# Moving the pools' subtraction of the token from VectorE to GpSimd, with rescaled operands, in an encoder layer

## The chip, the cores and the metric

The kernel runs on one core of one Trainium2 chip. The metric is the device time of one execution in microseconds (us), the median of several runs. One execution was also profiled, and all rows of the trace below come from that one. Engines: PE is TensorE, DVE is VectorE, ACT is ScalarE, POOL is GpSimd, SP issues transfers. Each engine works through its own queue in order. A difference of 0.2% is about 1.8 us here.

## The reference, cut to what matters

One layer on 512 tokens of 1024 channels, all in float32. The middle of it is a mixing block between two feed-forward blocks:

```python
h = h + 0.5 * swiglu(rms_norm(h, ffn1_norm[l]), ...)
u = rms_norm(h, mix_norm[l]) @ w_in[l]
q, k, v, pc = jnp.split(u, ...)          # 512 | 128 | 128 | 512 columns
a = window_attention(q, k, v, sink_logits[l])
p = multiscale_pool(pc, pool_w[l], pool_scale[l])
h = h + jnp.concatenate([a, p], axis=-1) @ w_out[l]
h = h + 0.5 * swiglu(rms_norm(h, ffn2_norm[l]), ...)
...
def multiscale_pool(u, w_pool, pool_scale):      # four groups of 128 channels, w = 2, 4, 8, 16
        means.append(0.5 * (win_mean(t - half, t + half - 1) + win_mean(t - half + 1, t + half)))
    d = (mean - uf).reshape(B, S, N_POOL_GROUPS, POOL_GROUP_WIDTH)
    y = jnp.einsum('bsgc,gcd->bsgd', d, w_pool.astype(jnp.float32)).reshape(B, S, POOL_WIDTH)
    return (y * pool_scale.astype(jnp.float32)).astype(u.dtype)
```

## The kernel before

Channels lie on the 128 partitions and the 512 tokens along a row. Every float32 product is made of three matmuls (`mm3`, lines 119 to 121): each operand is split into a rounded part and a rest, as `wh` and `wl` for weights and `pdh` and `pdl` for the pools. Weights stream from memory in units; ACT rounds (line 93), and for the two projections of the mixing block the rest is made by a negation (ACT at line 97 or POOL at line 99) and a transfer that POOL issues and that adds the raw weights (line 101).

The mixing block lies between about 376 and 515 us of the span. Its projections come in the order k and v, the pool of window 16, q0, the pool of window 8, q1, q2, q3, and the pools of window 4 and 2. I call a pool by its window: pool 16, pool 8, pool 4 and pool 2 (`gi` 3 to 0). A pool goes through these steps:

- `uu` (line 423): DVE takes the projected token off PSUM and multiplies it with the norm's factor.
- `widen` and `scale` (lines 430 to 439): POOL adds shifted copies, one step per doubling of the window, corrects a few columns at either edge, and adds the two half windows into `dd`.
- `less_token` (line 442): DVE forms `dd * 0.5 / w - uu`.
- `halves` (lines 446 and 447): ACT rounds `dd` into `pdh`, DVE subtracts for `pdl`.
- `pool_linear` (lines 460 to 464): PE multiplies with the pool's weights, ACT and DVE scale by `pool_scale` and split again.

These steps are put in a list per pool (`later`) and taken off one at a time, one after each step of the work that PE does meanwhile (`eased`); `AFTER` empty steps lie between the sum and the subtraction. The attention is woven in between: scores of a block of 128 queries on PE (lines 523 and 524), the row's extreme on DVE (line 525), the exponential on ACT (528), the division on POOL (535), transposes on PE (552), their split on ACT and DVE (556 and 557, `ph` and `pl`), products on PE (567 and 568). PSUM has eight banks, so the PE can run some eight scores ahead of DVE. The order in which instructions stand in each engine's queue is fixed when the program is built, by a scheduler that departs from the order of the code in places.

Of the kernel before, what the change touches and what calls it, by code (L numbers as in the profile page):

```python
# [11 lines left out]
ALU = mybir.AluOpType  # L12
# [3 lines left out]
S = 512  # L16
# [7 lines left out]
NEG = -1e30  # L24
F0 = 3
WARM = 10
AFTER = 11
EARLY = 12
LAG = 4
POOL_W = (2, 4, 8, 16)  # L30
PAD = 8
# [3 lines left out]
def encoder_layer(ctx: ExitStack, tc: tile.TileContext, xT, w1h, w1gu, w1d, win, wout, w2h, w2gu, w2d,  # L35
                  gains, gfin, sinks, poolw, pscale, cosT, sinT, edges, out):
    nc = tc.nc
# [8 lines left out]
    def cut(a, n):  # L46
        return small[:, a:a + n]
# [98 lines left out]
    nc.gpsimd.dma_start(sink[:, 0, :], sinks)  # L146
    psc = cut(40, 4)
    nc.gpsimd.dma_start(psc, pscale)
    ident = base.tile([P, P], F32, name="ident")
    make_identity(nc, ident)  # L150
    epsb = cut(48, 1)
# [171 lines left out]
    with tc.tile_pool(name="mix", bufs=1) as mp:  # L323
# [89 lines left out]
        later = []  # L413

        def pool_means(gi, ps):
            w = POOL_W[gi]
            half = w // 2
            e0 = 2 * (half - 1)
            uu = mp.tile([P, S + 128], F32, name="uu", tag="pl", bufs=3)[:, :S + 2 * PAD]
            n = S + 2 * PAD  # L420
            nc.gpsimd.memset(uu[:, :PAD], 0.0)
            nc.gpsimd.memset(uu[:, n - PAD:], 0.0)
            nc.vector.tensor_tensor(uu[:, PAD:PAD + S], ps, rstd, op=ALU.mult)
            box = {"cur": uu}

            def widen(step):
                m = n - 2 * step + 1
                cur = box["cur"]
                nxt = mp.tile([P, S + 128], F32, name="s1", tag="s1", bufs=2)
                nc.gpsimd.tensor_tensor(nxt[:, :m], cur[:, :m], cur[:, step:step + m], op=ALU.add)  # L430
                box["cur"] = nxt

            def scale():
                cur, o = box["cur"], PAD - half
                for a, e in ((o, e0), (o + S + 1 - half, e0 + half)):
                    nc.gpsimd.tensor_tensor(cur[:, a:a + half], cur[:, a:a + half], edge[:, e:e + half],
                                            op=ALU.mult)
                box["dd"] = mp.tile([P, S], F32, name="dd", tag="ph", bufs=3)
                nc.gpsimd.tensor_tensor(box["dd"], cur[:, o:o + S], cur[:, o + 1:o + 1 + S], op=ALU.add)  # L439

            def less_token():
                nc.vector.scalar_tensor_tensor(box["dd"], box["dd"], 0.5 / w, uu[:, PAD:PAD + S],
                                               op0=ALU.mult, op1=ALU.subtract)

            def halves():
                nc.scalar.copy(pdh[:, gi, :], box["dd"])
                nc.vector.tensor_tensor(pdl[:, gi, :], box["dd"], pdh[:, gi, :].bitcast(F32),
                                        op=ALU.subtract)

            wait = [lambda: None]  # L450
            steps = []
            while 1 << len(steps) < w:
                steps.append(lambda step=1 << len(steps): widen(step))
            later.append(steps + [scale] + (AFTER - len(steps)) * wait + [less_token, halves])

        def pool_linear(gi):
            while later[3 - gi]:
# [10 lines left out]
        def projected(gi):  # L468
            steps = project(pc[gi])
            last = steps.pop()  # L470
            return steps + [lambda: (last(), pool_means(gi, pc[gi]["ps"]))]
# [14 lines left out]
        nc.vector.tensor_tensor(sr, sr, rstd, op=ALU.mult)  # L486
        keys()
        pool_means(3, pc[3]["ps"])
        vT = mp.tile([P, 4, 4 * P], F32, name="vT", tag="sc", bufs=4).rearrange("p i c -> p (i c)")[:, :S]
        nc.vector.tensor_tensor(vT, bv["ps"], rstd, op=ALU.mult)  # L490
# [307 lines left out]
```

## Time and profile before

| what | value |
|---|---|
| median of 3 runs | 896.76 us (896.28 to 897.34) |
| the profiled execution | 895.57 us |
| its span, first to last instruction | 893.8 us |
| PE busy in the span | 872.9 us (98%) |
| DVE, ACT, POOL busy | 397.2, 320.2, 313.4 us |

The page shows PE busy in nearly every slice of the span; the two slices where it falls to seven tenths lie in the mixing block. The span is 1.8 us shorter than the time of its execution, and that execution is 1.2 us below the median.

### The profile page before, as it was taken

The numbers are of one execution on the slowest core, as the hardware profiler recorded it, in microseconds if no ns is written. First come the engines' busy times: TensorE is split into PE (matmuls) and PEld (weight loads), VectorE is DVE, ScalarE is ACT, GpSimd is POOL, SyncE is SP. The second block draws the span as 40 slices with busy tenths as digits, with TensorE's granted clock in tenths as the row PEclk, the third lists the DMA queues.
The fourth block names the chain that finished last, engine by engine and source line by source line (L and its number), as shares of the span: only waits on it lengthen the run. The fifth ranks groups of instructions, "written<-read, shape, count | busy, mean of one in ns | idle before, by whom it ended". The sixth has DMA issues, their size and how long they took to land.

```text
span 893.8 us, 9718 instructions
## 1 busy us (share of the span) xinstructions
PE 872.9 (98%) x3918; PEld 720.9 (81%) x3918; DVE 397.2 (44%) x505; ACT 320.2 (36%) x464; POOL 313.4 (35%) x274
## 2 busy tenths in 40 slices
PE   9999999999999999999779999999999999999996
PEld 7888888888888888778658888888888888888885
DVE  6444444444422221548697543444444444322225
ACT  7253223332221112754666542443332232211123
POOL 5086444444410000836643320663334444200004
PEclk9999999999999999999899999999999999999998
DMA  6422222222222223585613332222222222322202
GB/s 236 160 76 95 99 98 105 105 106 100 94 95 95 95 94 113 135 212 134 140 57 70 96 118 100 89 95 95 94 95 95 95 94 95 124 98 106 105 16 94
DMA packets 17276, 94.23 MB, mean 105 GB/s; under 512 B 2112, under 2 KB 2640, under 8 KB 8400
## 3 DMA queue, kind: packets, MB, share of 16 engines
q1 hardware_dynamic: 13104, 81.60, 25.6%
q0 software_dynamic: 2688, 9.46, 5.4%
q10 hardware_dynamic: 1440, 2.57, 0.9%
q8 instruction: 30, 0.49, 0.2%
q14 instruction: 14, 0.11, 0.0%
HBM read 82.08 MB, written 2.10 MB: 94 GB/s over the span
## 4 chain that ended last, share of the span: by engine, by line
PE 88%; POOL 4%; DVE 3%; DMA 2%; issue 2%; ACT 1%; DVEq 0%; ACTq 0%; POOLq 0%; SPq 0%
PE ps L119 28%; PE ps L120 28%; PE ps L121 28%; POOL s L430 1%; DMA raw<-in_win 1%; PE ps L552 1%; DVE yl L165 1%; PE ps L568 1%; DMA wl<-raw 1%; PE ps L567 1%; POOL wl L101 1%; DVE h L306 1%; DMA small<-in_gains 0%; POOL dd L439 0%; PE ps L660 0%
## 5 line engine op out<-in xcount | busy, mean ns | idle before, releaser
L93 ACT CAST wh<-raw 128x1024 fp32r<-128x1024 f32 (+2 forms) x153 | 156.3, 1024 | 406.9 <-PE ps L120 329.0
L103 DVE TENSOR_TENSOR wl<-raw,wh 128x1024 fp32r<-128x1024 f32 (+2 forms) x135 | 201.3, 1494 | 193.3 <-ACT wh L93 192.1
L119 PE MATMUL ps<-zh,wh 128*128 128x512 f32 x346 | 135.5, 392 | 0.0
L120 PE MATMUL ps<-zl,wh 128*128 128x512 f32 x346 | 135.1, 390 | 0.0
L121 PE MATMUL ps<-xh,wl 128*128 128x512 f32 x346 | 134.9, 390 | 0.0
L119 PE MATMUL ps<-xh,wh 128*128 128x512 f32 x346 | 134.8, 390 | 0.0
L121 PE MATMUL ps<-zh,wl 128*128 128x512 f32 x346 | 134.8, 390 | 0.0
L120 PE MATMUL ps<-xl,wh 128*128 128x512 f32 x346 | 134.6, 389 | 0.0
L213 POOL TENSOR_TENSOR t<-t,t 128x512 f32<-128x512 f32 x44 | 77.6, 1767 | 146.9 <-ACT t L212 146.9
L215 POOL TENSOR_TENSOR t<-t,rstd 128x512 f32<-128x512 f32 x44 | 61.2, 1395 | 99.3 <-DVE t L214 99.3
L214 DVE TENSOR_TENSOR t<-ps,t 128x512 f32<-128x512 f32 x44 | 30.4, 691 | 120.2 <-PE ps L121 108.2
L119 PEld LDWEIGHTS ps<-xh,wh 128*128 128x128 f32 x346 | 64.9, 188 | 14.0 <-ACT wh L93 0.3
L121 PEld LDWEIGHTS ps<-zh,wl 128*128 128x128 f32 x346 | 64.9, 188 | 13.8 <-issue 0.2
L121 PEld LDWEIGHTS ps<-xh,wl 128*128 128x128 f32 x346 | 64.9, 188 | 13.8 <-issue 0.2
L120 PEld LDWEIGHTS ps<-zl,wh 128*128 128x128 f32 x346 | 65.0, 188 | 13.5 <-issue 0.2
L120 PEld LDWEIGHTS ps<-xl,wh 128*128 128x128 f32 x346 | 64.9, 188 | 13.5
L119 PEld LDWEIGHTS ps<-zh,wh 128*128 128x128 f32 x346 | 65.0, 188 | 13.3
L211 DVE TENSOR_TENSOR t<-ps,rstd 128x512 f32<-128x512 f32 x44 | 30.2, 690 | 92.4 <-PE ps L121 75.9
L119 PE MATMUL ps<-a1h,wh 128*128 128x512 f32 x176 | 68.5, 389 | 0.0
L120 PE MATMUL ps<-a1l,wh 128*128 128x512 f32 x176 | 68.5, 389 | 0.0
L121 PE MATMUL ps<-a1h,wl 128*128 128x512 f32 x176 | 68.5, 389 | 0.0
L101 POOL DMA_DIRECT2D wl<-raw x18 | 15.7, 872 | 124.3 <-ACT wl L97 120.0
(191 smaller groups left out, 1291.3 us busy)
## 6 DMA issues: line engine op xcount, KB each, us to landing
raw<-in_w1gu SPq DMA_DIRECT2D x19, 1024.0 KB, 4.7
raw<-in_w2gu SPq DMA_DIRECT2D x19, 1024.0 KB, 4.8
raw<-in_w1d SPq DMA_DIRECT2D x11, 1024.0 KB, 4.8
raw<-in_w2d SPq DMA_DIRECT2D x11, 1024.0 KB, 4.7
wl<-raw POOLq DMA_DIRECT2D x18, 512.0 KB, 4.5
raw<-in_win SPq DMA_DIRECT2D x5, 1024.0 KB, 4.8
raw<-in_wout SPq DMA_DIRECT2D x4, 1024.0 KB, 5.2
raw<-in_w2h SPq DMA_DIRECT2D x4, 768.0 KB, 4.3
```

Of the source, the lines that this page charges most:

```text
L93: nc.scalar.copy(wh[:, c:c + m], src[:, c:c + m])
L101: nc.gpsimd.dma_start(wl[:, c:c + m], src[:, c:c + m], accum_op=ALU.add)
L103: nc.vector.tensor_tensor(wl[:, c:c + m], src[:, c:c + m], wh[:, c:c + m].bitcast(F32), op=ALU.subtract)
L119: nc.tensor.matmul(ps, lhsT=ah, rhs=bh, start=start, stop=False)
L120: nc.tensor.matmul(ps, lhsT=ah, rhs=bl, start=False, stop=False)
L121: nc.tensor.matmul(ps, lhsT=al, rhs=bh, start=False, stop=stop)
L165: nc.vector.scalar_tensor_tensor(xl[:, k, :], h[:, k, :], g, xh[:, k, :].bitcast(F32), op0=ALU.mult, op1=ALU.subtract)
L211: nc.vector.tensor_tensor(t1, pg, rstd, op=ALU.mult)
L213: nc.gpsimd.tensor_tensor(t2, t2, t1, op=ALU.mult)
L214: nc.vector.tensor_tensor(t1, pu, t2, op=ALU.mult)
L215: nc.gpsimd.tensor_tensor(t1, t1, rstd, op=ALU.mult)
L306: nc.vector.scalar_tensor_tensor(h[:, i, :], ps, 0.5, h[:, i, :], op0=ALU.mult, op1=ALU.add)
```

## The change

The subtraction of the token goes from DVE to POOL. [...] The pool's scale at the end is multiplied by `1 / (2 w)` instead, once, on four columns at the start. The subtraction stands directly behind the sum in the pool's list, and 22 steps lie between the sum and `halves` where there were 11 up to the subtraction (the widening steps count in both).

```diff
-AFTER = 11
+AFTER = 22
...
     nc.gpsimd.dma_start(psc, pscale)
+    for i, w in enumerate(POOL_W):
+        nc.gpsimd.tensor_scalar(psc[:, i:i + 1], psc[:, i:i + 1], 0.5 / w, 1.0, op0=ALU.mult, op1=ALU.mult)
...
             def less_token():
-                nc.vector.scalar_tensor_tensor(box["dd"], box["dd"], 0.5 / w, uu[:, PAD:PAD + S],
-                                               op0=ALU.mult, op1=ALU.subtract)
+
+                nc.gpsimd.tensor_scalar(uu[:, PAD:PAD + S], uu[:, PAD:PAD + S], 2.0 * w, 1.0,
+                                        op0=ALU.mult, op1=ALU.mult)
+                nc.gpsimd.tensor_tensor(box["dd"], box["dd"], uu[:, PAD:PAD + S], op=ALU.subtract)
...
-            later.append(steps + [scale] + (AFTER - len(steps)) * wait + [less_token, halves])
+            later.append(steps + [scale, less_token] + (AFTER - len(steps)) * wait + [halves])
```

Lines of the changed kernel are two higher from line 149 on and four higher from line 443 on. The queues move at three places.

The first place is ACT's queue behind the projection of q0 (`vv` is the values, `qq` the queries). Before:

```order
L97 ACTIVATE wl<-wh 128x1024
L395 ACTIVATE qq<-u 64x512 x2
L406 CAST vv<-ps 128x4x64
L446 CAST pdh<-dd 128x512
L93 CAST wh<-raw 128x1024
L446 CAST pdh<-dd 128x512
L97 ACTIVATE wl<-wh 128x1024
```

And after the change:

```order
L97 ACTIVATE wl<-wh 128x1024
L450 CAST pdh<-dd 128x512
L397 ACTIVATE qq<-u 64x512 x2
L408 CAST vv<-ps 128x4x64
L93 CAST wh<-raw 128x1024
L450 CAST pdh<-dd 128x512
L97 ACTIVATE wl<-wh 128x1024
```

The rounding of pool 16 now stands ahead of the queries q0. The rounding of pool 8 keeps its place.

The second place is DVE's queue at the first scores (`uu` here is pool 4's, the rows of line 525 are the extremes of the first scores). Before:

```order
L396 SCALAR_TENSOR_TENSOR qq<-u,qq 64x512 x2
L423 TENSOR_TENSOR uu<-ps,rstd 128x512
L525 ISA sc,st<-ps,mask,small 128x256
L525 ISA st 128x1
L525 ISA sc,st<-ps,mask,small 128x256
L525 ISA st 128x1
L442 SCALAR_TENSOR_TENSOR dd<-dd,uu 128x512
L525 ISA sc,st<-ps,mask,small 128x256
L525 ISA st 128x1
L447 TENSOR_TENSOR pdl<-dd,pdh 128x512
L525 ISA sc,st<-ps,mask,small 128x256
```

And after the change:

```order
L398 SCALAR_TENSOR_TENSOR qq<-u,qq 64x512 x2
L425 TENSOR_TENSOR uu<-ps,rstd 128x512
L529 ISA sc,st<-ps,mask,small 128x256
L529 ISA st 128x1
L529 ISA sc,st<-ps,mask,small 128x256
L529 ISA st 128x1
L529 ISA sc,st<-ps,mask,small 128x256
L529 ISA st 128x1
L451 TENSOR_TENSOR pdl<-dd,pdh 128x512
L529 ISA sc,st<-ps,mask,small 128x256
```

The subtraction is gone from between the second and the third extreme. The split `pdl` of pool 4, which needs the finished `dd`, still stands ahead of the fourth.

The third place is POOL's queue at pool 2 (line 535, later 539, is the attention's division, 439 and 441 the pool's sum). Before:

```order
L436 TENSOR_TENSOR s_2980<-s_2980,edge 128x1 x2
L535 TENSOR_SCALAR sc<-sc,st 128x384
L439 TENSOR_TENSOR dd<-s_2980 128x512
L535 TENSOR_SCALAR sc<-sc,st 128x384 x3
L516 COPY sc<-small 128x4
L535 TENSOR_SCALAR sc<-sc,st 128x384 x4
```

And after the change:

```order
L438 TENSOR_TENSOR s_2985<-s_2985,edge 128x1 x2
L539 TENSOR_SCALAR sc<-sc,st 128x384
L441 TENSOR_TENSOR dd<-s_2985 128x512
L539 TENSOR_SCALAR sc<-sc,st 128x384 x3
L445 TENSOR_SCALAR uu<-uu 128x512
L520 COPY sc<-small 128x4
L539 TENSOR_SCALAR sc<-sc,st 128x384
L447 TENSOR_TENSOR dd<-dd,uu 128x512
L539 TENSOR_SCALAR sc<-sc,st 128x384 x3
```

The scaling and the subtraction of pool 2 stand among the divisions, and four divisions now lie between the sum and the subtraction.

## Rows read from the trace of the kernel before

**Rows 1.** The page: span, and busy time of each engine.

```profile
span 893.8 us, 9718 instructions
...
PE 872.9 (98%) x3918; PEld 720.9 (81%) x3918; DVE 397.2 (44%) x505; ACT 320.2 (36%) x464; POOL 313.4 (35%) x274
```

**Rows 2.** Waits of PE from 370 to 520 us: total, times, longest.

```profile
PE ps L568 <- DVE pl L557: 4.9, 1, 4.9
PE ps L523 <- DVE st L525: 4.9, 2, 4.5
```

**Rows 3.** Timeline of PE: start, us, what, idle before and its releaser.

```profile
430.97 0.40 PE L121 MATMUL ps<-yh,wl 128*128 128x512 f32 x1
435.88 0.69 PE L523 MATMUL ps<-kk,qq 128*128 128x384 f32 x1 [4.51 <-DVE st L525]
...
437.25 0.69 PE L523 MATMUL ps<-kk,qq 128*128 128x384 f32 x1 [0.37 <-DVE st L525]
...
452.01 0.80 PE L568 MATMUL ps<-pl,vz 128*128 128x512 f32 x1 [4.92 <-DVE pl L557]
...
455.38 0.43 PE L567 MATMUL ps<-ph,vv 128*128 128x512 f32 x1
...
461.52 0.47 PE L119 MATMUL ps<-pdh,wh 128*128 128x512 f32 x1
...
470.50 0.39 PE L119 MATMUL ps<-pdh,wh 128*128 128x512 f32 x1
```

**Rows 4.** Timeline of DVE.

```profile
413.03 0.69 DVE L442 SCALAR_TENSOR_TENSOR dd<-dd,uu 128x512 f32<-128x512 f32 x1 [0.93 <-POOL dd L439]
...
417.45 1.40 DVE L396 SCALAR_TENSOR_TENSOR qq<-u,qq 64x512 fp32r<-64x512 f32 x2 [0.70 <-ACT qq L395]
...
428.50 0.69 DVE L423 TENSOR_TENSOR uu<-ps,rstd 128x512 f32<-128x512 f32 x1
...
434.73 0.69 DVE L442 SCALAR_TENSOR_TENSOR dd<-dd,uu 128x512 f32<-128x512 f32 x1 [4.73 <-POOL dd L439]
...
446.89 4.47 DVE L442 SCALAR_TENSOR_TENSOR dd<-dd,uu 128x512 f32<-128x512 f32 x1 [1.13 <-POOL dd L439]
...
461.29 0.61 DVE L525 CUSTOM_DVE_ANT_0 sc<-ps,mask,small 128x384 f32<-128x384 f32 x1
...
461.83 0.61 DVE L525 CUSTOM_DVE_ANT_0 sc<-ps,mask,small 128x384 f32<-128x384 f32 x1
```

**Rows 5.** Timeline of POOL.

```profile
9.08 1.34 POOL L176 TENSOR_TENSOR acc<-acc,sq 128x512 f32<-128x512 f32 x1 [5.38 <-ACT sq L175]
...
399.36 4.68 POOL L430 TENSOR_TENSOR s<-s 128x525 f32<-128x525 f32 x3
...
411.53 1.47 POOL L439 TENSOR_TENSOR dd<-s 128x512 f32<-128x512 f32 x1
...
433.65 1.04 POOL L439 TENSOR_TENSOR dd<-s 128x512 f32<-128x512 f32 x1
...
442.03 1.06 POOL L99 TENSOR_SCALAR wl<-wh 128x1024 fp32r<-128x1024 f32 x1
...
446.56 1.93 POOL L535 TENSOR_SCALAR sc<-sc,st 128x384 f32<-128x384 f32 x3
...
448.38 2.43 POOL L535 TENSOR_SCALAR sc<-sc,st 128x384 f32<-128x384 f32 x4
```

**Rows 6.** Timeline of ACT.

```profile
435.45 0.62 ACT L446 CAST pdh<-dd 128x512 fp32r<-128x512 f32 x1 [3.39 <-DVE dd L442]
...
458.94 0.68 ACT L462 ACTIVATE pdh<-ps,small 128x512 fp32r<-128x512 f32 x1
```

**Rows 7.** Stretches: busy time of each engine, granted clock of TensorE, DMA share, GB/s.

```profile
435.90:442.00 6.10, 5.73 (x16) 4.93 (x17) 5.90 (x24) 5.44 (x19) 3.69 (x8) 0.52 0.46 94
...
452.00:456.00 4.00, 3.99 (x11) 3.29 (x12) 4.00 (x7) 2.35 (x5) 0.00 (x0) 0.57 0.16 68
```

**Rows 8.** A stretch further on in the mixing block, same columns.

```profile
464.00:480.00 16.00, 16.00 (x90) 13.50 (x90) 12.83 (x36) 11.89 (x33) 9.00 (x18) 1.00 0.03 5
```

## The prediction, made before the changed kernel ran

> **What bounds the kernel now.** I read the page first. PE is busy for 872.9 of 893.8 us [rows 1], so at most 21 us of the span can be won, and only where PE stands still or runs slow. The waits of PE in the mixing block come next: two long ones, each behind DVE, 4.9 us for the products' `pl` and 4.9 us, in two pieces, for the extremes of the scores [rows 2]. In the timeline of PE they lie at 431.37 (the end of the row at 430.97) to 435.88, with 0.37 us more before 437.25, and before 452.01 [rows 3]. I call them the first and the second wait. The reader is to see in the timeline of DVE what held DVE there. At the first wait DVE stood at pool 4's subtraction for 4.73 us, until POOL had summed; the third extreme, which frees PE's bank, is queued behind it. At the second wait pool 2's subtraction took 4.47 us where the others take 0.69 [rows 4]. All of that time POOL ran divisions without a gap [rows 5].
>
> Behind each wait PE's clock falls: 0.52 of full speed granted from 435.9 to 442 and 0.57 from 452 to 456 [rows 7], that is, mostly 1.2 GHz instead of 2.4 after PE stood idle. From 464 to 480 us PE is busy all the time [rows 8]. So the question is when PE gets to the first matmul of the output projection, at 461.52, and from there to the common point at 470.50 [rows 3]. The nine us between hold the same matmuls in both kernels, in another order.
>
> The sum is of differences, against the profiled execution of 895.57 us (span 893.8 and 1.8 around it); the median is 1.19 us above it, and I add the same difference to the median. The measurement tells a difference from none at about 0.2%, 1.8 us.
>
> **Prices.** The change removes four DVE subtractions, 0.69 us each when quiet. It adds to POOL four scalings of 128x512 and four subtractions. A division of 384 columns takes 0.61 us (2.43 for four) and a scaling of 1024 takes 1.06 [rows 5], so 512 columns cost about 0.70 by their line. A two-input operation on POOL takes 1.04 when DVE is quiet (pool 4's sum) and 1.47 beside DVE (pool 8's) [rows 5]; both ends stay in the range. I take 1.04, because DVE now has nothing to do behind the sums but wait for them. The four scalings of a 128x1 column stand ahead of POOL's first sum of squares, before which POOL idles for 5.38 us until ACT has squared [rows 5]; I cost them at nothing, and without that cover they would be less than 4 x 0.70 = 2.8 us on POOL alone.
>
> **First part: pools 16 and 8.** POOL now does two scalings and two subtractions more before pool 8's `dd` is final: 2 x 0.70 + 2 x 1.04 = 3.48 us. Against that the widening adds of pool 16 took 1.56 each (4.68 for three) where 1.04 is the quiet price [rows 5], and they may go quiet as DVE and ACT now stand at pool 16's rounding, queued ahead of the queries. I take back one such excess, 0.55: 2.93 us. What follows is shorter than before. Before, from the sum's end (411.53 + 1.47 = 413.00) to the end of the queries q1 on DVE (417.45 + 1.40 = 418.85) went 5.85 us [rows 4, 5]: DVE's subtraction and then the whole rotation. Now the rotation has already begun, and behind pool 8's subtraction only the rounding on ACT (0.62 [rows 6]), `pdl` and the last add of the rotation (0.69 each), ACT's queries (the 0.70 of idle) and 1.40 on DVE are left [rows 4]: 4.10. So the queries q1 end 2.93 - 1.75 = 1.2 us later. The rotations of q2 and q3 and pool 4's `uu` (428.50 [rows 4]) follow one behind the other on DVE and shift alike. Bounds: all four adds go quiet, nothing is late (0); none does and both subtractions cost 1.47, 4.34 - 1.75 = 2.6 us late. The transfer for the last projection's weights, which ACT's negation behind pool 8's rounding releases, is late too; PE would wait under 2 us there, and that lies inside the first wait.
>
> **Second part: pool 4 and the first scores.** The third extreme no longer waits, so PE does one score more. But the fourth stands behind `pdl` of pool 4, and `pdl` behind ACT's rounding, and that behind POOL. From the sum's end (433.65 + 1.04 = 434.69) to PE's score at 437.25 went 2.56 us [rows 3, 5]. Now 0.70 and 1.04 are added on POOL and 0.69 is gone from DVE: 1.05 us more. The wait is not removed: it moves by one score, and it ends 1.2 + 1.05 = 2.25 us later than before. DVE is idle there, so the quiet price holds.
>
> **Third part: pool 2 and the products.** In times of before (to which 2.25 is added): POOL reaches the end of three divisions at 448.38, then scales (0.70), divides once (0.61) and subtracts (1.04): 450.73. ACT rounds `pdh` (0.62) and then the fourth `ph` (as much): 451.95, and PE's fourth product can go at 452.0 where it went at 455.38 [rows 3, 5]. So 3.4 us come back here, not 4.9: ACT now waits where DVE did. Part of it is lost again. Pool 2's own linear map needs `pdl`, which DVE does behind five extremes: from 452.0 DVE has six operations of at most 0.69 and five extremes 0.54 apart (461.29, 461.83 [rows 4]), 6.8 us, so PE gets `pdl` at 458.8. PE's two matmuls, some 0.5 us, ACT's scaling (0.68 [rows 6]) and the hops bring the output projection to 460.1, against 461.52: 1.4 us earlier. From there the same matmuls follow.
>
> **Sum:** +2.25 - 1.4 = +0.85 us; with the clock left as it is, because one long wait goes from 4.9 to some 6.5 us and the other from 4.9 to two shorter ones, I forecast about 0.7 more than before: 896.3 for a profiled execution, 897.5 us for the median, no change that can be measured.
>
> **Rivals.** *Faster, the waits hidden (0.13).* POOL goes quiet, nothing is late in the first part, and extremes and split run so early that only the fourth `ph` counts: PE's 6.1 us from 455.38 to 461.52 [rows 3] shrink by their idle and slow time to some 5.3 and start at 452.0, so 457.3, 4.2 earlier; with the 1.05 of pool 4, 3.2 us are won: 893.6. For it speaks that DVE is free of its 4.47 us; against it, that `pdl` stands where it stands in DVE's queue. *Faster, the second wait simply goes (0.05):* 4.92 us and 4.0 x 0.43 = 1.7 us of slow clock [rows 3, 7], 6.6 in all, 890.2. Against it speaks that ACT must round pool 2 ahead of the fourth `ph`.
>
> *Slower, POOL beside DVE (0.31).* The subtractions of pools 16 and 8 run beside the queries and the values on DVE at 1.47, as pool 8's sum did [rows 5]; the first part is late by 2.6 and pool 4 by 1.05, 3.65 together, and pool 2's path is 0.43 longer, so only 1.0 comes back: +2.65, 899.4, and up to 1.5 more if the clock also falls behind the new waits. It decides from 2.2 us of delay in the first part on.
>
> The slower rival has a page behind it. The Trainium skill (GPSIMD Engine Reference, Engine selection) keeps elementwise work on VectorE, since two-input operations on GpSimd are about half as fast; this case's rows show 1.04 against 0.69, half as long again rather than double. By the page an estimate for one subtraction is 1.38, and four of them on the path make the sum some 1.4 us longer, 898.9. The same page (Key points) says that GpSimd shares its SBUF interfaces with VectorE and collides with DVE instructions of two SBUF inputs; the 4.47 us beside POOL's divisions agree.
>
> **Chances.** The forecast has 0.51, with its own range from 895.0 to 898.5. Faster by more than 0.2%: 0.13 + 0.05 and a little of the forecast's lower edge, 0.19. Slower: 0.31. Within: 0.50. Eight times in ten the time should lie from 893.9 to 900.3; this leaves out the fastest rival, part of the other and the slowest tail.
>
> **What the profile would show.** Right: DVE without line 442's rows; the long wait of PE at the scores one score later, over 6 us, ending 2 us later in the span; ACT idle behind POOL's subtraction of pool 16, 4 and 2; PE waiting at the fourth product on ACT's `ph` and before the output projection on `pdl` or `pdh`. POOL's scaling at 0.7 and its subtraction near 1.04. Wrong: a first wait that ends no later than before, which the quiet POOL would do; no wait for pool 2's `pdl`; or subtractions of 1.5 us and more.

## The result: 4.6 us slower, and the profile after

The changed kernel takes 901.36 us (median of 4 runs, 900.73 to 901.93) against 896.8 for the kernel before (4 runs): a ratio of 1.0051, 95% interval 1.0033 to 1.0068. The forecast was 897.5, with a range up to 900.3. The profiled execution took 900.73 us.

The page of the changed kernel, the lines that answer to [rows 1]:

```profile
span 899.0 us, 9715 instructions
...
PE 875.9 (97%) x3918; PEld 723.8 (81%) x3918; DVE 393.4 (44%) x501; ACT 321.0 (36%) x464; POOL 321.1 (36%) x286
```

PE has the same 3918 matmuls, but is busy 3.0 us longer: the same work ran at a lower clock for longer (the mean granted clock of the execution is 0.987, against 0.992 before). DVE lost its four subtractions, and POOL got twelve instructions: four on the columns of `pool_scale`, and for each pool a multiplication of the token by `2 w` and its subtraction from the unscaled sum. The waits of PE in the mixing block (370 to 525 us; total, times, longest), against [rows 2]:

```profile
PE ps L527 <- DVE st L529: 6.9, 1, 6.9
PE ps L571 <- ACT ph L560: 2.5, 1, 2.5
PE ps L121 <- DMA wl<-raw: 2.2, 2, 1.1
PE ps L120 <- DVE pdl L451: 2.1, 1, 2.1
PE ps L119 <- ACT pdh L466: 0.8, 1, 0.8
```

The first wait grew from 4.9 to 6.9 us. The second shrank from 4.9 to 2.5, and two new ones came, for pool 2's `pdl` and for its scaled `pdh`. Of the two waits for weights (`wl<-raw`), one was there before; the other ends at 422.68, ten us ahead of the first wait, which takes it up, as the prediction had it. They lie in the timeline of PE as follows, against [rows 3]:

```profile
432.93 0.34 PE L528 MATMUL ps<-kl,qq 128*128 128x384 f32 x1
440.13 0.69 PE L527 MATMUL ps<-kk,qq 128*128 128x384 f32 x1 [6.86 <-DVE st L529]
...
455.32 0.50 PE L571 MATMUL ps<-ph,vv 128*128 128x512 f32 x1 [2.46 <-ACT ph L560]
...
462.85 0.53 PE L120 MATMUL ps<-pdl,pwh 128*128 128x512 f32 x1 [2.10 <-DVE pdl L451]
...
464.63 0.80 PE L119 MATMUL ps<-pdh,wh 128*128 128x512 f32 x1 [0.83 <-ACT pdh L466]
...
475.69 0.40 PE L119 MATMUL ps<-pdh,wh 128*128 128x512 f32 x1
```

The first wait ends 2.88 us later than before (440.13 against 437.25), the output projection starts 3.11 later (464.63 against 461.52), and the common point is 5.19 later (475.69 against 470.50). That is the whole difference of the spans, 5.2. So 2.9 us were lost before the first wait ended, 0.2 on the way to the output projection, and 2.1 in the nine us behind it, where the prediction saw nothing. The stretches of the changed kernel show what that is (length; busy time and count of PE, PEld, DVE, ACT, POOL; granted clock; DMA share; GB/s), against [rows 7]:

```profile
440.00:446.00 6.00, 5.87 (x18) 5.48 (x19) 5.66 (x25) 5.89 (x20) 4.78 (x10) 0.50 0.00 1
...
456.40:459.80 3.40, 3.40 (x12) 3.19 (x11) 2.59 (x6) 2.10 (x5) 0.00 (x0) 0.50 0.00 0
459.80:463.20 3.40, 1.30 (x9) 0.90 (x7) 3.40 (x11) 3.07 (x9) 0.00 (x0) 1.00 0.00 0
463.20:470.00 6.80, 5.97 (x21) 4.43 (x20) 4.19 (x12) 3.91 (x11) 4.69 (x9) 0.50 0.01 2
470.00:475.69 5.69, 5.69 (x31) 4.56 (x30) 3.67 (x8) 3.17 (x7) 0.19 (x1) 1.00 0.00 0
```

In the mixing block the clock stood at 1.2 GHz (0.50) in three stretches, where the kernel before had two. The new one, 463.2 to 470, is the longest and lies where before PE ran at full clock [rows 8]. Ahead of it PE had 1.30 us of work in 3.40, because of the wait of 2.10.

### The profile page after: what moved, and what is told of

Same layout as the page of the kernel before. It is cut to its first block, busy times and chain, and to the rows that moved or that the text cites. A ratio compares the mean times of both kernels' runs of the same rounds, so it can differ in the third digit from the quotient of the medians.

```text
span 899.0 us, 9715 instructions
## 1 busy us (share of the span) xinstructions
PE 875.9 (97%) x3918; PEld 723.8 (81%) x3918; DVE 393.4 (44%) x501; ACT 321.0 (36%) x464; POOL 321.1 (36%) x286
## 4 chain that ended last, share of the span: by engine, by line
PE 87%; POOL 5%; DVE 3%; DMA 2%; ACT 2%; issue 1%; DVEq 0%; ACTq 0%; POOLq 0%; SPq 0%
PE ps L119 28%; PE ps L121 28%; PE ps L120 28%; POOL s L432 1%; DMA raw<-in_win 1%; PE ps L556 1%; DVE yl L167 1%; DMA wl<-raw 1%; POOL dd L447 1%; PE ps L571 1%; POOL wl L101 1%; DVE h L308 0%; PE ps L572 0%; POOL dd L441 0%; DMA small<-in_gains 0%
```

## The theories and what tells them apart

All kernels behind the common point are alike: from there to the end of the span it is 423.2 to 423.3 us in every trace. So three distances, taken inside one trace, say where a kernel gains or loses: from the first matmul of the norm's sums (385.64 us before, 385.76 after) to the end of the first wait; from there to the first matmul of the output projection; from there to the common point. For the kernel before these are 437.25 - 385.64 = 51.61, 24.27 and 8.98.

| kernel | median us | ratio to before, 95% | to the end of the first wait | to the output projection | to the common point |
|---|---|---|---|---|---|
| before | 896.8 | | 51.61 | 24.27 | 8.98 |
| changed | 901.36 | 1.0033 to 1.0068 | 54.37 | 24.50 | 11.06 |
| 1: no scaling | 897.6 | 1.0005 to 1.0022 | 52.88 | 22.42 | 11.35 |
| 2: only pool 2 | 897.38 | 1.0002 to 1.0020 | 51.55 | 25.11 | 10.56 |
| 3: all but pool 2 | 899.15 | 1.0021 to 1.0048 | 54.54 | 24.20 | 8.97 |
| 4: zero matmuls, late | 897.51 | 1.0006 to 1.0024 | 54.39 | 23.68 | 8.35 |
| 5: split 11 behind | 897.61 | 1.0003 to 1.0023 | 54.71 | 22.80 | 8.99 |
| 6: before, split 22 | 900.08 | 1.0029 to 1.0055 | 51.62 | 28.06 | 10.01 |
| 7: before, zero matmuls | 892.86 | 0.9945 to 0.9969 | 51.63 | 21.73 | 8.97 |
| 8: only pool 2, zero matmuls | 893.36 | 0.9953 to 0.9977 | 51.68 | 22.76 | 8.38 |
| 9: split 11, zero matmuls | 894.35 | 0.9975 to 0.9993 | 54.55 | 19.71 | 8.89 |
| 10: only pool 2, split 11, zero matmuls | 891.29 | 0.9935 to 0.9963 | 51.49 | 20.23 | 8.92 |
| 11: before, zero matmuls, first wait | 891.83 | 0.9936 to 0.9961 | 51.84 | 19.38 | 8.97 |
| 12: before, zero matmuls, second wait | 895.08 | 0.9982 to 1.0000 | 51.61 | 23.69 | 9.00 |

The distances are of one profiled execution each; that of the kernel before is 1.2 us under its median, so differences of the traces come out about that much larger than those of the medians. Part of the spread lies ahead of the mixing block: the norm's first matmul comes at 385.37 to 385.95 us in ten of the fourteen traces and at 386.78 to 387.13 in the other four (experiments 4, 5, 10 and 11). The distances leave that out, the medians don't.

**Theory A**: POOL's chain (scale, subtract) is longer than DVE's was, and PE waits for its end. **Theory B**: the split 22 steps behind, which puts pool 2's `pdl` behind the extremes on DVE, is what costs. **Theory C**: the clock that falls behind the new waits is the larger part.

## The experiments

**1. Without the scaling.**

```diff
-                nc.gpsimd.tensor_scalar(uu[:, PAD:PAD + S], uu[:, PAD:PAD + S], 2.0 * w, 1.0,
-                                        op0=ALU.mult, op1=ALU.mult)
```

> The changed kernel without POOL's four scalings of the token by 2w (this leaves out the factor 2w, so the pools are computed otherwise); PE, ACT and DVE keep the order of the changed kernel. Theory A (POOL's longer chain is what PE waits for): the scalings of pools 16, 8 and 4 (1.05 + 0.95 + 0.62 us) stand ahead of the first wait and that of pool 2 (0.62) ahead of the fourth product; the first wait ends about 2.6 us earlier, the whole is 898.5 us (897.5 to 899). Theory B (the later rounding and the new order are the cause, POOL's price is hidden): within 0.7 us of the changed kernel, 901.4. Theory C (the clock is the larger part, and shorter waits keep it up): below 897.

Measured: 897.6 us, 3.8 less than the changed kernel, in the range of theory A. The timeline of PE:

```profile
438.77 0.69 PE L527 MATMUL ps<-kk,qq 128*128 128x384 f32 x1 [6.16 <-DVE st L529]
...
459.64 0.50 PE L120 MATMUL ps<-pdl,pwh 128*128 128x512 f32 x1 [2.10 <-DVE pdl L451]
...
461.19 0.79 PE L119 MATMUL ps<-pdh,wh 128*128 128x512 f32 x1 [0.83 <-ACT pdh L466]
```

The first wait ends 1.5 us earlier (52.88 against 54.37) and not 2.6: where the scalings go, the widening adds take longer (three of pool 16 took 4.69 us, and 1.51 + 2.76 with the scaling among them), and with the other adds they eat 1.1 of the 2.6. Another 2.1 us come in the second distance, from pool 2. There more has changed than the scaling: in POOL's queue the subtraction stands directly behind three divisions, and the fourth, which stood ahead of it, comes behind it. So the 2.1 us are not the scaling's price alone. But the waits for `pdl` and `pdh` are still there, with the same 2.10 and 0.83, and so is the long last distance, 11.35. POOL's price is real, and it is not what makes the last two us.

**2 and 3. Pool 2 alone, and all but pool 2.** The pools in `ON` take the new way, the others the old one with 11 steps.

```diff
+ON = (0,)
...
+                if gi in ON:
+                    nc.gpsimd.tensor_scalar(uu[:, PAD:PAD + S], uu[:, PAD:PAD + S], 2.0 * w, 1.0,
+                                            op0=ALU.mult, op1=ALU.mult)
+                    nc.gpsimd.tensor_tensor(box["dd"], box["dd"], uu[:, PAD:PAD + S], op=ALU.subtract)
+                else:
+                    nc.vector.scalar_tensor_tensor(box["dd"], box["dd"], 0.5 / w, uu[:, PAD:PAD + S],
+                                                   op0=ALU.mult, op1=ALU.subtract)
```

> Only pool 2's subtraction on POOL and its rounding 22 steps behind; pools 16, 8 and 4 as in the kernel before. Theory A with the clock: first and second part as before; the fourth product comes earlier, but PE then waits for pool 2's pdl and pdh and runs at the lower level behind them, so 2.3 us are lost (5.2 less the 2.9 that the changed kernel was late at the first wait): 899.1 us. The prediction's third part without a fall of the clock: 1.4 us are won, 895.4 us.

> Pools 16, 8 and 4 on POOL and rounded 22 steps behind; pool 2 as in the kernel before. Theory A: the first wait ends 2.9 us later as in the changed kernel, the second wait is the old one: 896.8 + 2.9 = 899.7 us. Rival (the delay of the first wait is made up at the second, because pool 2's sums don't depend on it): about 897.5.

Measured: 897.38 and 899.15 us. With all but pool 2 the loss stands in the first distance alone (54.54, and 24.20 and 8.97 as before), and the median is near theory A's 899.7. With pool 2 alone the first distance is that of before, and the other two are 0.84 and 1.58 us longer: in the trace 2.4 us, as expected, in the medians only 0.6, far from the 899.1 expected. The profiled execution is 0.5 us above its median and that of the kernel before 1.2 below its own, which makes up nearly all of the difference. The profiled execution shows a mean granted clock of 0.989, as one other of this kernel does, and eight show 0.990 to 0.993: in most of them TensorE spent less time at 1.2 GHz than in the trace. So what pool 2 alone costs stays open between 0.6 and 2.4 us. Both readings are against the 1.4 us of gain that the prediction's third part gave to pool 2. And as pools 16, 8 and 4 are split 22 steps behind in the third experiment too, without harm to the last distance, it is pool 2's split that matters there.

**4. PE kept at work in the late waits.** Matmuls that add zero (one of their operands is the mask's middle block, which is all zero) go into the same bank: 8 ahead of the fourth product and 8 inside pool 2's linear map. Ahead of the output projection stand 3 of the kernel's warming matmuls, whose result the first matmul of the projection overwrites. None adds anything to a sum.

```diff
+    def idle_turns(ps, n, stop=False):
+        for j in range(n):
+            nc.tensor.matmul(ps[:, 0:P], lhsT=ones, rhs=box0["zero"], start=False, stop=stop and j == n - 1)
...
+                if n == 0 and x == 3:
+                    idle_turns(po[g], 8)
...
+            if gi == 0:
+                idle_turns(pp, 8)
...
+                if d == 0 and i == 0 and bh is pdh:
+                    keep_awake(ws[1], 3)
```

> The changed kernel with matmuls that add zero while PE waits for the fourth product and for pool 2's pdl, and 3 of the warming ones before the output projection; the first wait as it is. If the clock's fall behind these waits costs time (theory C): the stretch from the first matmul of the output projection, 6.8 us at 1.2 GHz, is nearly 2.7 us shorter: 898.7 us (898 to 899.5). If PE's speed there is hidden by ACT and DVE: 901.4 within 0.7.

Measured: 897.51 us, 3.85 less, and below the range expected of theory C (898 to 899.5). The stretch from the output projection to the common point:

```profile
465.20:473.55 8.35, 8.35 (x47) 6.85 (x47) 6.26 (x15) 5.96 (x15) 3.96 (x9) 1.00 0.00 0
```

The clock is 1.00 and the stretch 8.35 us instead of 11.06: 2.7 less, the number that theory C gave. Here the split and POOL's chain are those of the changed kernel, so this is time that the clock took: 2.1 us of it, if one goes by the kernel before, where the same distance takes 8.98 at full clock. The scheduler also moved one product, two transposes and one rounding on ACT, and the other 0.6 may be theirs. The middle distance is 0.82 shorter; in this trace the clock is 1.00 from 456 us on, so the fall behind the wait for `ph` is gone too. The first wait and its slow stretch were left alone (54.39 against 54.37).

**5. The split 11 steps behind again**, subtraction and scaling on POOL.

```diff
-AFTER = 22
+AFTER = 11
```

> The changed kernel with the split 11 steps behind again (subtraction and scaling stay on POOL). Only the last stretch is ordered otherwise: pool 2's pdl stands ahead of the extremes on DVE and its linear map ahead of the scores on PE. If the later split caused the third loss (PE's wait for pdl, 2.1 us, for pdh, 0.8 us, and the lower clock behind them, some 2 us): the first wait ends as in the changed kernel, both later waits go, 897 us (896 to 898). If POOL's price alone is the cause: within 0.7 of 901.4.

Measured: 897.61 us, 3.75 less, as expected. The timeline of PE, and the stretch behind the output projection:

```profile
441.74 0.69 PE L527 MATMUL ps<-kk,qq 128*128 128x384 f32 x1 [6.88 <-DVE st L529]
...
456.94 0.50 PE L571 MATMUL ps<-ph,vv 128*128 128x512 f32 x1 [2.74 <-ACT ph L560]
...
464.00 0.63 PE L556 MATMUL ps<-ident,sc 128*128 128x128 f32 x4 [1.29 <-DVE st L529]
464.54 0.47 PE L119 MATMUL ps<-pdh,wh 128*128 128x512 f32 x1
```

```profile
464.54:473.53 8.99, 8.98 (x49) 6.95 (x49) 8.34 (x23) 7.16 (x21) 4.91 (x10) 1.00 0.01 2
```

(All times of this trace are 1.3 us higher than those of the changed kernel, since the norm's first matmul comes at 387.03; the distances don't depend on it.) The first wait is as late as in the changed kernel and the wait for `ph` is there, but no wait for `pdl` or `pdh` follows. A wait of 1.29 us for DVE stands ahead of the output projection, and the clock behind it is 1.00 all the same; the last distance is that of before, 8.99. The middle one is 1.47 us shorter than before: this is the size of the gain that the prediction expected of the third part, though it expected it with `pdl` behind the extremes.

**6. The kernel before with subtraction and split 22 steps behind.**

```diff
-AFTER = 11
+AFTER = 22
```

> The kernel before (DVE subtracts) with the subtraction and the split 22 steps behind the sum instead of 11. If the later split costs time by itself: both old waits stay, and PE waits for pool 2's pdl (2.1) and pdh (0.8) with a fall of the clock behind them besides, 4 to 5 us lost less what pool 2's path had in hand (0.6): 899 to 901 us. If the later split only hurts beside POOL's chain: 896.8 within 0.7.

Measured: 900.08 us, as expected. DVE subtracts as ever, POOL does nothing new, and 3.3 of the 4.6 us are there. The timeline of PE:

```profile
451.84 0.79 PE L568 MATMUL ps<-pl,vz 128*128 128x512 f32 x1 [4.98 <-DVE pl L557]
...
463.60 0.50 PE L120 MATMUL ps<-pdl,pwh 128*128 128x512 f32 x1 [2.10 <-DVE pdl L447]
...
465.12 0.80 PE L119 MATMUL ps<-pdh,wh 128*128 128x512 f32 x1 [0.78 <-ACT pdh L462]
```

The old second wait stands (4.98), and behind it the same two new ones, 2.10 and 0.78. The middle distance is 3.79 us longer than before, the last one 1.03. This and the fifth experiment decide between theories A and B: the later split makes most of the loss, with POOL (3.75) or without (3.3); POOL without the later split costs 0.85 us (0.3 to 2.1 by the interval). Theory C is no rival of B, since the split brings the waits behind which the clock falls. By the fourth experiment the clock takes at least the 2.1 us of the last distance, and at most the 3.5 that all three distances won back there, of the 5.2 of the trace; whether that is the larger part stays open.

**7 to 12. Zero matmuls in other kernels.** In all but the twelfth they stand behind `F`, the last score that PE does ahead of the first wait: 16 of them, and 24 in the ninth, where the wait is longer and comes one score later. In the seventh and twelfth 20 stand between the first product's two matmuls, in the ninth and tenth 10 ahead of the fourth product; the eighth has those of the fourth experiment besides.

```diff
-                nc.tensor.matmul(ps[:, :w], lhsT=q, rhs=kl[:, g, ks], start=False, stop=True)
+                nc.tensor.matmul(ps[:, :w], lhsT=q, rhs=kl[:, g, ks], start=False, stop=(n, g, i) != F)
+                if (n, g, i) == F:
+                    idle_turns(ps, 16, True)
...
+                if n == 0 and x == 0:
+                    idle_turns(po[g], 20)
                 nc.tensor.matmul(po[g], lhsT=vz[:, b, g, :], rhs=pl, start=False, stop=b == hi - 1)
```

> The kernel before with matmuls that add zero in its two long waits (16 behind a score, 20 between the first product's two matmuls). If the clock behind a wait is what costs: the stretches at 1.2 GHz of 6 and 3.4 us give back up to 3.0 and 1.7 us, less where another engine then ends last: 893 to 895 us. If PE's speed behind its waits is hidden by DVE and ACT: 896.8 within 0.7.

> Only pool 2 on POOL (as in the second experiment), with zero matmuls in the first wait, ahead of the fourth product and inside pool 2's linear map. If the clock took what the shorter second wait gave: 892 to 894.5 us, faster than both kernels. If it is bound by the chain through DVE: 896 to 897.5.

> All four subtractions on POOL, split 11 steps behind (as in the fifth experiment), 24 zero matmuls in the first wait and 10 ahead of the fourth product. Clock held: the 6 us at 1.2 GHz behind the first wait shrink by up to 3, the rest by about 1; 897.6 - 4 = 893.6 us (893 to 895). If the end of the first wait, which POOL's chain sets, decides all that follows: 896 to 897.6.

> Only pool 2 on POOL, split 11 steps behind, 16 zero matmuls in the first wait and 10 ahead of the fourth product. If the subtraction of pool 2 on POOL is worth anything once split and clock don't cost: below the kernel before with zero matmuls, 891.5 to 892.5 us. If not: 892.9 or up to 1 us more.

> The kernel before with 16 zero matmuls in the first wait only. By the clock: up to 3.0 us of the 6 us at 1.2 GHz behind it come back, 894 us, less what the second wait, which is set by POOL's divisions and not by PE, takes again; if the second wait starts from the scores, all is kept. If the order that the scheduler changes (POOL sums pool 2 ahead of the divisions) gives it instead: the second wait is shorter in the trace.

> The kernel before with 20 zero matmuls in the second wait only; POOL's order is unchanged. By the clock: 3.4 us at 1.2 GHz give back 1.7, less 0.6 where DVE's extremes then end last: 895.4 us (894.8 to 896.2). If PE's speed there is hidden: 896.8 within 0.7.

Measured: 892.86, 893.36, 894.35, 891.29, 891.83 and 895.08 us. The seventh and the tenth are 0.1 and 0.2 us under their ranges, the eleventh 2 us under its number, and the others inside. All are faster than the kernel before (the interval of the twelfth just touches 1); the tenth and eleventh, some 5 us faster, do best, and stand too near each other to tell them apart. The twelfth is the cleanest look at the clock, since POOL's order is that of before. Its stretch behind the second wait, then DVE's subtraction of pool 2:

```profile
452.00:456.00 4.00, 2.93 (x9) 1.49 (x10) 3.29 (x6) 2.11 (x4) 0.00 (x0) 1.00 0.16 66
```

```profile
446.82 4.48 DVE L449 SCALAR_TENSOR_TENSOR dd<-dd,uu 128x512 f32<-128x512 f32 x1 [1.14 <-POOL dd L446]
```

The clock is 1.00 instead of 0.57 [rows 7], the output projection comes 0.58 us earlier (23.69 against 24.27), and the rest of the 1.7 is taken by waits for ACT and DVE. So in the traces the clock behind the second wait is worth less than the clock behind the last ones. The medians can't confirm it: they differ by 1.4 us, with an interval from 0 to 1.6.

The eleventh missed its expectation on the good side, 891.83 for 894. Its second alternative shows: the scheduler, with longer work on PE, put POOL's sum of pool 2 ahead of all divisions of 384 columns. POOL, then DVE and PE in that trace:

```profile
446.43 1.04 POOL L446 TENSOR_TENSOR dd<-s 128x512 f32<-128x512 f32 x1
447.44 2.80 POOL L544 TENSOR_SCALAR sc<-sc,st 128x384 f32<-128x384 f32 x4
```

```profile
447.50 0.69 DVE L449 SCALAR_TENSOR_TENSOR dd<-dd,uu 128x512 f32<-128x512 f32 x1 [1.03 <-POOL dd L446]
```

```profile
448.50 0.50 PE L576 MATMUL ps<-ph,vv 128*128 128x512 f32 x1 [1.73 <-ACT ph L565]
```

DVE's subtraction took 0.69 us and not 4.47, and of the second wait 1.73 us are left, for ACT. How the 4.6 us that this kernel gains divide between that order and the clock behind the first wait is not separated: no run had the new order without the zeros. The seventh has the new order too, so its gain is not shown to be the clock's alone either.

## Why the prediction was wrong

**First part (pools 16 and 8) and second part (pool 4): right in mechanism, 0.6 us too small.** The long wait moved by one score, and ends 2.88 us later where 2.25 was forecast. POOL in the changed kernel, against [rows 5], and the queries q1 on DVE:

```profile
400.70 1.05 POOL L445 TENSOR_SCALAR uu<-uu 128x512 f32<-128x512 f32 x1
...
406.65 1.29 POOL L447 TENSOR_TENSOR dd<-dd,uu 128x512 f32<-128x512 f32 x1
...
410.98 0.95 POOL L445 TENSOR_SCALAR uu<-uu 128x512 f32<-128x512 f32 x1
...
415.02 1.29 POOL L447 TENSOR_TENSOR dd<-dd,uu 128x512 f32<-128x512 f32 x1
...
434.04 0.62 POOL L445 TENSOR_SCALAR uu<-uu 128x512 f32<-128x512 f32 x1
...
435.00 0.88 POOL L101 DMA_DIRECT2D wl<-raw  x1
435.62 1.34 POOL L441 TENSOR_TENSOR dd<-s 128x512 f32<-128x512 f32 x1
437.04 1.26 POOL L447 TENSOR_TENSOR dd<-dd,uu 128x512 f32<-128x512 f32 x1
...
451.48 0.62 POOL L445 TENSOR_SCALAR uu<-uu 128x512 f32<-128x512 f32 x1
452.16 0.19 POOL L520 COPY sc<-small 128x4 f32<-128x4 f32 x1
...
452.87 1.26 POOL L447 TENSOR_TENSOR dd<-dd,uu 128x512 f32<-128x512 f32 x1
```

```profile
418.99 1.41 DVE L398 SCALAR_TENSOR_TENSOR qq<-u,qq 64x512 fp32r<-64x512 f32 x2 [0.70 <-ACT qq L397]
```

A scaling cost 0.62 where DVE stood still (434.04) or had an operand in PSUM (451.48), and 1.05 and 0.95 beside DVE's work on two operands in SBUF; 0.70 lies between. The subtraction cost 1.26 to 1.29, not 1.04, even at 437.04, where DVE was idle; the quiet price of a sum was the wrong row for it. The Trainium skill (GPSIMD Engine Reference, Engine selection) has two-input operations on GpSimd at about half of VectorE's speed; 1.26 against 0.69 agrees with that better than the 1.5 times that I read off the sums.

So the two scalings and two subtractions ahead of pool 8's end cost 4.58 us and not 3.48. POOL's adds and sum gave back 1.27 (I had taken 0.55, and 1.56 - 1.04 is 0.52): pool 8 was done at 416.31, 3.31 later than the sum at 413.00, where 2.93 was forecast. From there to the end of q1 on DVE went 4.09 us, as forecast (4.10). So q1 ended 1.55 us later and not 1.2, and pool 4 added 1.33 and not 1.05. The hand-over of pool 4 from POOL to ACT to DVE came as forecast: ACT's rounding, then DVE's `pdl`.

```profile
438.33 0.62 ACT L450 CAST pdh<-dd 128x512 fp32r<-128x512 f32 x1 [4.67 <-POOL dd L447]
```

```profile
438.99 0.69 DVE L451 TENSOR_TENSOR pdl<-dd,pdh 128x512 fp32r<-128x512 f32 x1 [7.02 <-ACT pdh L450]
```

**Third part (pool 2): the places right, the sum wrong.** The fourth product waits for ACT's `ph` at 455.32 (454.25 forecast), and PE for `pdl` behind the extremes, as forecast. The output projection was to come 1.4 us earlier than the first wait allowed, and came 0.2 later. The fourth product was 1.07 late on its forecast, 0.63 of it from the first wait. Of the other 0.44, 0.22 is POOL's dearer subtraction and 0.19 the copy at 452.16, which the sum left out. `pdl` was 1.80 late (462.85 against 458.8 + 2.25), 0.73 more. The output projection was 2.28 late (464.63 against 460.1 + 2.25), 0.48 more, since the two matmuls ahead of it took 0.95 us (462.85 to 463.80) where I had set some 0.5. In all 1.65. The 0.73 are DVE's in the main: of its six operations one had to wait for ACT, and ACT for a product of PE, in the stretch at 1.2 GHz from 456.4 (DVE, then ACT):

```profile
457.97 0.69 DVE L577 TENSOR_TENSOR rtmp<-ps,rtmp 64x512 f32<-64x512 f32 x1 [0.78 <-ACT rtmp L576]
```

```profile
457.36 0.58 ACT L576 COPY rtmp<-ps 64x512 f32<-64x512 f32 x1 [0.76 <-PE ps L572]
```

**The step that failed: "From there the same matmuls follow", with the sum made "with the clock left as it is".** The same matmuls did follow, but the clock was not left: the last distance took 11.06 us instead of 8.98, 2.1 us. With the 1.65 of the third part and the 0.63 of the first wait this makes the 4.3 us between 0.85, the sum, and 5.19. I had the waits at the output projection in hand, and in the profile of before I had the fall behind each wait [rows 7]; I did not put the one behind the other, because I set the shorter second wait against the longer first one. The fourth experiment shows that the clock took this time, and the fifth and sixth that the later split brought the waits ahead of it. All that the prediction had named as signs of being right came, the waits for `ph`, `pdl` and `pdh` among them (only POOL's prices were off); none of the signs looked at the clock behind these waits, so they could not tell this result from the forecast.

**The rivals.** The slower one, POOL beside DVE, named the right sign and, with its 1.5 us for the clock, came to 900.9, near the 901.36. That is luck in part: the 3.65 us that it set for the first wait were 2.88, its subtractions at 1.47 took 1.26 to 1.29, and the 1.0 us that was to come back at pool 2 did not. Its mechanism was a part: with POOL's work and the split 11 steps behind the kernel is 0.85 us slower. Neither of the faster ones happened. What no rival had is that the later split, which the prediction took as a detail of the third part, costs 3.3 us without any help.

## What to carry to other kernels

When an edit lets a half of some operand be made later, look for the queue in which it then stands, and put the wait that follows at the next place where nothing else is late; there a wait can cost its own length and the slow clock behind it (here 2.1 us), while the fall behind an earlier wait was in the traces mostly swallowed by other engines (0.6 us for the 4 us at 0.57). Test such a change one part at a time: one number (22 for 11) was most of this loss. And a wait that can't be removed can be filled with matmuls that add zero: the kernel before came down to 891.8 us, with the help of a new order on POOL, and the one with all four subtractions on POOL and the split 11 steps behind to 894.4.

## What the runs showed of the hardware that I had not expected

- DVE's subtraction of pool 2, with two inputs in SBUF, took 4.47 or 4.48 us in each of four traces (before, third, sixth, twelfth) in which POOL's run of divisions had begun 0.3 us ahead of it, and 0.69 in the seventh and eleventh, in which POOL went on with divisions for 2.8 us but began only 0.06 us ahead. The Trainium skill (GPSIMD Engine Reference, Key points) says that GpSimd shares its SBUF interfaces with VectorE and contends with its instructions of two SBUF inputs; the traces agree, and add that divisions beside it were not enough: in these six the order in which the two began goes with the time, though no run changed that order alone. POOL's start times are rough, so which of the two began first in the fast case isn't certain.
- POOL's subtraction into its own first input took 1.26 us with DVE idle, where the sum of the same size took 1.04 [rows 5]. The sum at 435.62 took 1.34, but began 0.26 us ahead of the end of the row before it. Why the subtraction takes longer stays open.
- Behind a wait of 2.10 us the clock fell to half for 6.8 us (463.2 to 470, with the wait of 0.83 inside), in which PE worked 5.97 us: as much as behind the wait of 6.86, with 5.87 us of work at 0.50 from 440 to 446. Behind the wait of 1.29 in the fifth experiment it did not fall.
